# Four instead of three K tile pairs per block as seven products in the up projection, with the squared rectification on ScalarE and earlier transposes

## The chip, the cores and the metric

The kernel runs on one core of one Trainium2 chip. The metric is device time in microseconds (us). A core has TensorE (PE; its weight loads are listed as PEld), VectorE (DVE), ScalarE (ACT), GpSimd (POOL) and SyncE (SP), each with its own stream of instructions; here SP only issues DMAs. The engines hand work to each other by semaphores.

## What is computed

One encoder block for 256 tokens of width 2048, all in 32-bit floats: an input projection, two kinds of attention, an output projection with a layer norm, and a feed-forward part with a second layer norm. The change lies in the first half of the feed-forward part:

```python
x = _layer_norm(DEEPNORM_ALPHA * x + mix, ln1_g[l], ln1_b[l])
h = jnp.square(jax.nn.relu(x @ w_up[l])) @ w_down[l]      # w_up 2048 x 8192, w_down 8192 x 2048
x = _layer_norm(DEEPNORM_ALPHA * x + h, ln2_g[l], ln2_b[l])
```

## The kernel before

**Number format.** A 32-bit value is used as a sum of two rounded halves, hi and lo, and a product becomes three matmuls: hi·hi, hi·lo, lo·hi. A weight arrives by DMA in a raw tile of 2048 columns (two K tiles of 128 rows, a "pair"). ACT writes the rounded hi half of 1024 columns (line 389) and DVE then subtracts it from the raw value to get lo (line 390). The hi and lo tiles lie in five slots (NSLOT); the raw tiles in three buffers (NRAW), so the load of pair j+3 waits until the last split of pair j has read its buffer.

**The up projection.** Its 8192 columns are worked off in eight blocks of 1024. Block 0 goes by single tiles of 128 columns (ft 0 to 7). While ft 3, 4 and 5 end, DVE and ACT also prepare, once for all blocks, sums of the tokens' halves for each pair that will be treated as seven products (lines 1058, 364 to 369). Blocks 1 to 7 take eight pairs each, with the tokens as the stationary side and 512 columns at a time. An ordinary pair (pair_products) is 24 matmuls: two K tiles, two token halves, two column halves, three parts. A pair of the list UP_SEVEN (seven_products) is computed with seven instead of eight sub-products in the manner of Strassen and Winograd, 21 matmuls. For this DVE first forms sums of the weights' quarters (lines 400 to 402, weight_sums), and three and a half tiles of 1024 are split instead of two. Block 1 does this with pairs 3 and 5, blocks 2 to 7 with pairs 3, 5 and 6. Below, the two splits of an ordinary pair 4 are called 4.0 and 4.1, and the four of a seven-product pair 3 are 3a to 3d (3d is half as wide).

**PSUM.** A block has four accumulators of its own (cb) and, for the seven products, four more (mb, allocated at its first seven-product pair). The two groups of four banks change roles from block to block. The transposes of a block's result go to the banks that held its cb, and these are then the banks of the next block's mb.

**The end of a block.** After the last seven-product pair up_gather copies the four mb banks with ACT and adds them up with DVE (lines 1098 to 1108). up_finish then treats four quarters i of the result. For each, ACT copies the quarter's cb bank to memory (1120, "own"), DVE adds it to the gathered quarter (1121; in block 7 straight from PSUM, 1123), and one DVE instruction rectifies and squares (1124). After four empty steps PE transposes each quarter (1137) and ACT copies it back to where the down projection will read it (1131, back).

**Order of the work.** The order within each engine is written out by hand: the program emits the instructions in sequence and each engine runs its own in that order. After each group of matmuls unit() is called. It first advances every generator of the list side (up_gather and up_finish are such generators, and each yield is one step), and then emits up to two weight pieces. A split needs a free slot: it is emitted once the slot five splits earlier has been released by its matmuls. The weight sums need none. An ordinary pair has four units (after each K tile and token half), a seven-product pair also four (after each of its splits a to d). up_finish starts within pair 7, at the unit after 7.1's first token half; its four quarters are the units up to 0.0 of the next block, and the transposes come at the units from 1.1 (first half) to 2.0 (second half).

The lines that put the steps of a quarter into one unit are these:

```python
for i in range(4):
    ...
    nc.scalar.copy(c, pb)
    nc.vector.tensor_add(g, g, c)
    ...
    nc.vector.scalar_tensor_tensor(g, g, 0.0, g, op0=ALU.max, op1=ALU.mult)
    yield
for _ in range(4):
    yield
```

Of the kernel before, what the change touches and what calls it, by code (L numbers as in the profile page):

```python
# [11 lines left out]
AF = mybir.ActivationFunctionType  # L12
ALU = mybir.AluOpType

P = 128
# [24 lines left out]
STORED = (12, 9, 22, 25, 4, 7)  # L40


UP_PAIRS = (3, 5, 6)
UP_SEVEN = ((), (3, 5)) + 6 * (UP_PAIRS,)
NHELD = 4
STAGE_AT = 24
# [34 lines left out]
def kernel(  # L81
# [19 lines left out]
    nc = tc.nc  # L101
# [364 lines left out]
    for b in range(1, 8):  # L466
        j_block.append([])
        for kp in range(8):
            j_block[b].append(up_pair(b, kp))
            if b == 1 and kp in (2, 6):  # L470
                i = (2, 6).index(kp)
# [384 lines left out]
    pts = {}  # L856
# [174 lines left out]
    for i in range(2):  # L1031
        t = work.tile([P, 2048], F32R, tag="big", name=f"us{i}", bufs=2)
        up_sums += [sums_view(t[:, a:a + 1024]) for a in (0, 1024)]
    rest = []
    for ft in range(NSPLIT, NFT):
# [5 lines left out]
        for p in range(ft == NSPLIT, 2):  # L1041
# [7 lines left out]
            if p == 1:  # L1049
                up_evac(ft, pb)  # L1050
                i = ft - 3
                if rest:
                    rest.pop()()
                if 0 <= i < len(UP_PAIRS):

                    k = slice(2 * UP_PAIRS[i], 2 * UP_PAIRS[i] + 2)
                    xs = spare_flat[:, 0:512].rearrange("p (k t) -> p k t", k=2)
# [20 lines left out]
    def seven_products(job, x, k, sums, cb, mb, first, last):  # L1078
        for a, w, o, pb, alone in ((("x", 1, 0), 0, 0, cb[0][0], False), (("s", 3), 0, 512, cb[0][1], False),
                                   (("x", 0, 0), 1, 0, mb[0], True), (("s", 1), 1, 512, mb[1], True),  # L1080
                                   (("s", 0), 2, 0, mb[2], True), (("s", 2), 2, 512, mb[3], True),
                                   (("x", 1, 1), 3, 0, cb[1][0], False)):
            use(job, w + 1)
            if a[0] == "x":
                h, l = (x[:, k + a[1], i * S + a[2] * P:i * S + (a[2] + 1) * P] for i in range(2))
            else:
                h, l = (sums[:, a[1], i] for i in range(2))
            hi, lo = job.hi[w][:, o:o + 512], job.lo[w][:, o:o + 512]
            for x_part, w_part, fst, lst in ((h, hi, True, False), (h, lo, False, False), (l, hi, False, True)):
                nc.tensor.matmul(pb, x_part, w_part, start=alone and first and fst, stop=alone and last and lst)  # L1090
            if o or w == 3:
                free(job, (w,))
                unit()
# [16 lines left out]
    def up_finish(b, cb, tag, seven):  # L1110

        r = rr[b // 4][:, b % 4 * 8:b % 4 * 8 + 8]
        own = r.rearrange("p f t -> p (f t)")
        for i in range(4):
            g, pb = gathered[i], cb[i // 2][i % 2]
            if not seven:
                nc.scalar.copy(g, pb)
            elif b < 7:
                c = own[:, i * 512:(i + 1) * 512]
                nc.scalar.copy(c, pb)  # L1120
                nc.vector.tensor_add(g, g, c)
            else:
                nc.vector.tensor_add(g, g, pb)
            nc.vector.scalar_tensor_tensor(g, g, 0.0, g, op0=ALU.max, op1=ALU.mult)
            yield
        for _ in range(4):
            yield
        pts = []

        def back(i):  # L1130
            nc.scalar.copy(r[:, i % 2 * 4:i % 2 * 4 + 4, i // 2 * P:(i // 2 + 1) * P],
                           pts[i].rearrange("p (f t) -> p f t", f=4))

        for i in range(4):
            pts.append(tag(f"ut{b}{i}"))
            for f in range(4):
                nc.tensor.transpose(pts[i][:, f * P:(f + 1) * P], gathered[i][:, f * P:(f + 1) * P], ident)  # L1137
            if b < 7:
                back(i)
            yield  # L1140
        if b == 7:
            for i in (0, 2):
                back(i)
                back(i + 1)
                yield

    for b in range(1, 8):
        tag, other_tag = (bank, acc) if b % 2 else (acc, bank)
        cb = [[tag(f"u{b}{tb}{j}") for j in range(2)] for tb in range(2)]
        mb = None  # L1150
        for n in range(8):
            job = j_block[b][n]
            if b == 7 and n == 7:
                r_split(0)
            if n in UP_SEVEN[b]:
                if mb is None:
                    mb = [other_tag(f"v{b}{j}") for j in range(4)]
                last = n == UP_SEVEN[b][-1]
                seven_products(job, x1hl, 2 * n, up_sums[UP_PAIRS.index(n)], cb, mb, n == UP_SEVEN[b][0], last)
                if last:  # L1160
                    side.append(up_gather(mb))
            else:
                pair_products(job, x1hl, 2 * n, cb, n == 0, n == 7,
                              up_finish(b, cb, tag, bool(UP_SEVEN[b])) if n == 7 else None)
# [51 lines left out]
    for p in range(2):  # L1216
        cb = [[(acc, bank)[p](f"d{p}{tb}{j}") for j in range(2)] for tb in range(2)]
        mb = None
        for n, pair in enumerate(pairs[p][:32 if p == 0 else 32 - NHELD]):
            b = pair // 2  # L1220
            if n % 2 == 0:
                i = n // 2 + 1
# [166 lines left out]
```

## Time and profile before

| what | value |
|---|---|
| time, median of 3 runs | 1112.53 us (1112.09 to 1113.03) |
| span of the profiled execution | 1110.6 us; the median lies 1.9 us above it |
| busy: PE, DVE, ACT | 99%, 81%, 55% of the span |
| granted TensorE clock | 0.999 |
| blocks 1 to 7 of the up projection | from 461.19 to 763.55 us |
| DMA | 217.08 MB, 195 GB/s mean |

The profile is one execution, with times from the span's start. In a timeline a row has its start, its duration, the engine and line, the operation with the names of what it writes and reads, and a count; in brackets stands how long the engine had been idle before it and what ended that. Rows that follow each other closely overlap a little, since an instruction starts while its predecessor drains: the cost of one in a full queue is the distance between starts. The chain of waits is the run of work that ended last, in order of time, and pauses between its pieces are work of other lines too short to be listed.

### The profile page before, as it was taken

Reading aid. Unit: us, or ns where it says so; the run is one execution under the profiler, and the core shown is the slowest. Engines: PE = TensorE matmul, PEld = TensorE weight load, DVE = VectorE, ACT = ScalarE, POOL = GpSimd, SP = SyncE. Lnnn points to the kernel's source line nnn. Section 1 sums busy time; section 2 is a strip of 40 time slices with the busy share of each in tenths; the row PEclk is TensorE's granted clock in tenths of the full one; section 3 lists DMA queues with packets and bytes.
Section 4 is the critical chain, followed back from the end, with each engine's and each line's share of the span. In section 5 each row is a group of like instructions: output and inputs, shape, how many; then the busy total and the mean of one; then the engine's idle time right before and its main releaser. Section 6 shows DMA issues by size and latency. Waiting matters only on the chain.

```text
span 1110.6 us, 13644 instructions
## 1 busy us (share of the span) xinstructions
PE 1102.9 (99%) x5193; PEld 921.7 (83%) x5193; DVE 901.0 (81%) x1198; ACT 613.8 (55%) x793; POOL 9.6 (1%) x18
## 2 busy tenths in 40 slices
PE   9999999999999999999999999999999999999997
PEld 8888888888888889888888888888888888888885
DVE  6676684666656777898998999899999998999886
ACT  4445664535453446455656656656666673665650
POOL 0000000000000000000000000000000000000000
PEclk9999999999999999999999999999999999999999
DMA  8655365444465554566656756755656665656672
GB/s 306 222 205 192 119 228 184 145 168 161 144 258 197 199 198 152 189 216 207 222 166 213 221 158 193 221 168 180 223 191 195 204 213 196 215 189 200 204 251 104
DMA packets 92561, 217.08 MB, mean 195 GB/s; under 512 B 4177, under 2 KB 62545, under 8 KB 84433
## 3 DMA queue, kind: packets, MB, share of 16 engines
q1 hardware_dynamic: 92064, 215.64, 57.7%
q8 instruction: 40, 0.66, 0.2%
q10 hardware_dynamic: 432, 0.59, 0.2%
q14 instruction: 25, 0.20, 0.1%
HBM read 214.12 MB, written 2.10 MB: 195 GB/s over the span
## 4 chain that ended last, share of the span: by engine, by line
PE 96%; DVE 2%; DMA 1%; issue 0%; ACT 0%; POOL 0%; DVEq 0%; ACTq 0%; POOLq 0%
PE d L302 20%; PE u L302 18%; PE r L302 16%; PE o L302 8%; PE v L1090 5%; PE m L302 5%; PE s L1090 4%; PE u L1090 4%; PE d L1090 3%; PE up L734 2%; PE pu L734 2%; PE ut L1137 1%; PE pv L302 1%; PE up L740 1%; PE pu L740 1%; PE pq L302 1%
## 5 line engine op out<-in xcount | busy, mean ns | idle before, releaser
L302 PE MATMUL d<-hi_wd,rhl 128*128 128x512 f32 x664 | 182.9, 390 | 0.0
L389 ACT CAST hi_wu<-raw_wu 128x1024 fp32r<-128x1024 f32 x112 | 118.1, 1058 | 116.6 <-DVE raw_wu L401 57.9
L389 ACT CAST hi_wd<-raw_wd 128x1024 fp32r<-128x1024 f32 x125 | 130.0, 1052 | 75.8 <-PE d L302 33.5
L390 DVE TENSOR_TENSOR lo_wd<-raw_wd,hi_wd 128x1024 fp32r<-128x1024 f32 x125 | 148.6, 1220 | 18.2 <-ACT hi_wd L389 17.4
L302 PE MATMUL u<-hi_wu,x1hl 128*128 128x512 f32 x576 | 162.7, 393 | 0.0
L390 DVE TENSOR_TENSOR lo_wu<-raw_wu,hi_wu 128x1024 fp32r<-128x1024 f32 x112 | 133.3, 1220 | 23.4 <-ACT hi_wu L389 22.6
L302 PE MATMUL r<-hi_ret,xhl 128*128 128x512 f32 x512 | 147.1, 397 | 0.0
L302 PEld LDWEIGHTS d<-hi_wd,rhl 128*128 128x128 f32 x664 | 124.3, 188 | 25.7
L302 PEld LDWEIGHTS u<-hi_wu,x1hl 128*128 128x128 f32 x576 | 106.4, 188 | 20.9
L302 PEld LDWEIGHTS r<-hi_ret,xhl 128*128 128x128 f32 x512 | 93.9, 188 | 18.2
L302 PE MATMUL d<-lo_wd,rhl 128*128 128x512 f32 x332 | 102.6, 389 | 0.1
L191 DVE TENSOR_TENSOR lo_ret<-raw_ret,hi_ret 128x1024 fp32r<-128x1024 f32 x64 | 75.7, 1220 | 23.9 <-ACT hi_ret L190 23.7
L302 PE MATMUL u<-lo_wu,x1hl 128*128 128x512 f32 x288 | 88.9, 390 | 0.0
L302 PE MATMUL r<-lo_ret,xhl 128*128 128x512 f32 x256 | 79.4, 391 | 0.0
L190 ACT CAST hi_ret<-raw_ret 128x1024 fp32r<-128x1024 f32 x64 | 64.9, 1051 | 16.4 <-PE r L302 12.2
L302 PEld LDWEIGHTS d<-lo_wd,rhl 128*128 128x128 f32 x332 | 62.2, 188 | 13.4 <-DVE lo_wd L390 0.6
L302 PEld LDWEIGHTS u<-lo_wu,x1hl 128*128 128x128 f32 x288 | 54.1, 188 | 11.4
L302 PE MATMUL o<-hi_wo,mix 128*128 128x512 f32 x208 | 57.1, 392 | 0.0
L302 PEld LDWEIGHTS r<-lo_ret,xhl 128*128 128x128 f32 x256 | 48.1, 188 | 10.4
L191 DVE TENSOR_TENSOR lo_wo<-raw_wo,hi_wo 128x1024 fp32r<-128x1024 f32 x26 | 31.2, 1222 | 19.6 <-ACT hi_wo L190 18.9
L302 PEld LDWEIGHTS o<-hi_wo,mix 128*128 128x128 f32 x208 | 38.7, 188 | 7.8
L302 PE MATMUL m<-hi_mla,xhl 128*128 128x512 f32 (+1 forms) x168 | 42.5, 363 | 0.0
(297 smaller groups left out, 1908.6 us busy)
## 6 DMA issues: line engine op xcount, KB each, us to landing
raw_wu<-in_w_up SPq DMA_DIRECT2D x64, 1024.0 KB, 5.7
raw_wd<-in_w_down SPq DMA_DIRECT2D x64, 1024.0 KB, 5.5
raw_ret<-in_w_ret SPq DMA_DIRECT2D x32, 1024.0 KB, 4.8
raw_wo<-in_w_out SPq DMA_DIRECT2D x16, 1024.0 KB, 4.8
raw_mla<-in_w_mla SPq DMA_DIRECT2D x14, 672.0 KB, 4.7
raw_qk<-in_w_qk SPq DMA_DIRECT2D x8, 640.0 KB, 3.9
row<-in_ln_rows SPq DMA_DIRECT2D x4, 1024.0 KB, 4.7
raw_uv<-in_w_uv SPq DMA_DIRECT2D x2, 1024.0 KB, 4.7
```

The costliest lines, as they stand in the source:

```text
L190: nc.scalar.copy(hi[:, o:e], r)
L191: nc.vector.tensor_sub(lo[:, o:e], r, hi[:, o:e].bitcast(F32))
L302: nc.tensor.matmul(accs[j][:, :w], x_part, w_part[:, a:a + w], start=first and fst and i == 0, stop=last and lst and i == len(steps) - 1)
L389: nc.scalar.copy(h, src)
L390: nc.vector.tensor_sub(l, src, h.bitcast(F32))
L734: nc.tensor.matmul(pb, hi[:, a:a + P], hl[:, k0 + i], start=first and i == ks[0], stop=last and i == ks[-1])
L740: nc.tensor.matmul(pb[:, 0:S], lo[:, a:a + P], hl[:, k0 + i, 0:S], start=False, stop=last and i == ks[-1])
L1090: nc.tensor.matmul(pb, x_part, w_part, start=alone and first and fst, stop=alone and last and lst)
L1137: nc.tensor.transpose(pts[i][:, f * P:(f + 1) * P], gathered[i][:, f * P:(f + 1) * P], ident)
```

## The change

A pair 2 is added to the list of seven-product pairs, so blocks 2 to 7 have four of them (2, 3, 5, 6) and block 1 still has 3 and 5. The sums of the tokens are prepared for four pairs, at ft 3 to 6. In up_finish DVE's instruction of line 1124 is replaced by an ACT instruction that rectifies in place, at the same point of the program, and the copy back after the transposes becomes an ACT instruction that squares. Two of the four empty steps go, so the transposes are emitted two units sooner, from 1.0 (first half) to 1.1 (second half).

```diff
-UP_PAIRS = (3, 5, 6)
+UP_PAIRS = (2, 3, 5, 6)
 UP_SEVEN = ((), (3, 5)) + 6 * (UP_PAIRS,)
...
                 nc.vector.tensor_add(g, g, c)
             else:
                 nc.vector.tensor_add(g, g, pb)
-            nc.vector.scalar_tensor_tensor(g, g, 0.0, g, op0=ALU.max, op1=ALU.mult)
+            nc.scalar.activation(g, g, AF.Relu)
             yield
-        for _ in range(4):
+        for _ in range(2):
             yield
         pts = []

         def back(i):
-            nc.scalar.copy(r[:, i % 2 * 4:i % 2 * 4 + 4, i // 2 * P:(i // 2 + 1) * P],
-                           pts[i].rearrange("p (f t) -> p f t", f=4))
+            nc.scalar.activation(r[:, i % 2 * 4:i % 2 * 4 + 4, i // 2 * P:(i // 2 + 1) * P],
+                                 pts[i].rearrange("p (f t) -> p f t", f=4), AF.Square)
```

## The prediction

> **What bounds the kernel now.** The page comes first.
>
> ```profile
> span 1110.6 us, 13644 instructions
> PE 1102.9 (99%) x5193; PEld 921.7 (83%) x5193; DVE 901.0 (81%) x1198; ACT 613.8 (55%) x793; POOL 9.6 (1%) x18
> ```
>
> PE is always busy, so a matmul less is time less, as long as DVE keeps up. The chain of waits, in order of time, gives the price of a matmul and the length of a block.
>
> ```profile
> 477.51 1.36 PE u L1090 x6
> ...
> 492.47 20.40 PE u L302 x90
> ...
> 628.01 14.96 PE u L302 x66
> 643.41 1.40 PE u L302 x6
> 645.25 1.39 PE u L302 x6
> ...
> 651.66 1.36 PE u L1090 x6
> ...
> 671.38 14.96 PE u L302 x66
> ```
>
> 66 matmuls in 14.96 us are 0.2267 us each. Pair 7 begins at 628.01 and again at 671.38: a block takes 43.37 us. The four short pauses (643.41 + 1.36 to 645.25: 0.48) are the transposes, 1.9 us in all; 183 matmuls of 0.2267 are 41.5, and together that is the block: no wait of PE is left in it. The windows view tells how near DVE is in this stretch.
>
> ```profile
> 608.29:651.66 43.37, 43.37 (x201) 35.92 (x200) 39.16 (x43) 27.00 (x34) 0.00 (x0) 1.00 0.64 194
> ```
>
> The third pair of columns is DVE: 39.16 of 43.37 us. What it spends them on is in its timeline.
>
> ```profile
> 611.92 1.22 DVE L400 TENSOR_TENSOR t<-raw_wu 128x1024 f32<-128x1024 f32 x1
> ...
> 614.51 2.35 DVE L390 TENSOR_TENSOR lo_wu<-raw_wu,hi_wu 128x1024 fp32r<-128x1024 f32 x2
> ...
> 618.52 1.22 DVE L400 TENSOR_TENSOR t<-raw_wu 128x1024 f32<-128x1024 f32 x1
> ...
> 621.11 2.35 DVE L390 TENSOR_TENSOR lo_wu<-raw_wu,hi_wu 128x1024 fp32r<-128x1024 f32 x2
> ...
> 625.12 4.63 DVE L390 TENSOR_TENSOR lo_wu<-raw_wu,hi_wu 128x1024 fp32r<-128x1024 f32 x4
> ...
> 633.22 1.23 DVE L390 TENSOR_TENSOR lo_wu<-raw_wu,hi_wu 128x1024 fp32r<-128x1024 f32 x1 [1.06 <-ACT hi_wu L389]
> 634.36 0.69 DVE L1105 TENSOR_TENSOR rr<-rr 128x512 f32<-128x512 f32 x1
> ...
> 635.69 0.69 DVE L1121 TENSOR_TENSOR rr<-rr 128x512 f32<-128x512 f32 x1
> 636.41 0.69 DVE L1124 SCALAR_TENSOR_TENSOR rr<-rr 128x512 f32<-128x512 f32 x1
> 637.02 0.69 DVE L1108 TENSOR_TENSOR rr<-rr 128x512 f32<-128x512 f32 x1
> ...
> 645.13 0.69 DVE L401 TENSOR_TENSOR raw_wu<-raw_wu,t 128x512 f32<-128x512 f32 x1
> ```
>
> A lo costs 1.135 (four in 4.63, whose last drains 0.09), so an ordinary pair 2.27. Weight sums cost 2.59 (611.92 to 614.51), a whole seven-product pair 6.60 (611.92 to 618.52). An add of up_finish with its rectification costs 1.33 (635.69 to 637.02), two adds of up_gather as much (634.36 to 635.69).
>
> **The sum of busy time.** On PE the fourth pair saves 3 matmuls in each of six blocks: 6 x 3 x 0.2267 = 4.1 us; a block without waits would be 42.7. On DVE a block was 5 x 2.27 + 3 x 6.60 + 4 x 1.33 + 2.7 of up_gather = 39.2, as measured. Afterwards it is 4 x 2.27 + 4 x 6.60 + 4 x 0.66 (the add alone) + 2.7 = 40.8: the four rectifications given away (2.7) pay for most of the pair (4.3). On this count DVE has 1.9 us to spare per block, where it had 4.2, and the change gains 4.1. The count leaves out the order.
>
> **The wait that is added.** In up_finish ACT now does own copy 0, rectification 0, own copy 1, rectification 1 and so on, and rectification i needs DVE's add i, while add i+1 needs own copy i+1, which stands behind rectification i. Until now ACT ran through these copies without waiting for DVE. ACT's timeline at the same block end:
>
> ```profile
> 629.25 1.05 ACT L389 CAST hi_wu<-raw_wu 128x1024 fp32r<-128x1024 f32 x1 [0.82 <-DMA raw_wu<-in_w_up]
> ...
> 632.11 1.08 ACT L389 CAST hi_wu<-raw_wu 128x1024 fp32r<-128x1024 f32 x1
> 633.05 1.10 ACT L1120 COPY rr<-u 128x512 f32<-128x512 f32 x2
> ...
> 638.93 1.06 ACT L389 CAST hi_wu<-raw_wu 128x1024 fp32r<-128x1024 f32 x1 [1.66 <-PE u L302]
> 645.94 1.05 ACT L389 CAST hi_wu<-raw_wu 128x1024 fp32r<-128x1024 f32 x1 [5.95 <-DVE raw_wu L401]
> 646.89 1.06 ACT L1131 COPY rr<-ut 128x512 f32<-128x512 f32 x2
> ```
>
> The last two rows show what an ACT queue behind a DVE wait looks like: the first transpose was over before PE went on at 643.41, but its copy back ran at 646.89, behind a hi split that waited 5.95 us for weight sums. Handovers cost little: DVE's L401 ends at 645.82 and ACT starts at 645.94 (0.12); ACT's split ends at 633.19 and DVE starts at 633.22 (0.03). The own copies take 0.5 each in the queue, and about 0.6 until the result is there. A rectification isn't in the trace; the nearest rows of ScalarE and of the instruction replaced are these.
>
> ```profile
> L613 ACT ACTIVATE vg<-vg 128x512 f32<-128x512 f32 x4 | 2.5, 633 | 0.0
> ...
> L1124 DVE SCALAR_TENSOR_TENSOR rr<-rr 128x512 f32<-128x512 f32 x28 | 19.4, 692 | 1.0
> ```
>
> I take 0.63, or 0.5 in a full queue. The Trainium skill, ScalarE: Activation LUTs, Rules for kernel authors, sends relu to VectorE, which it says is up to about 3 times faster in bf16. By that rule a rectification would take some 2 us here, an estimate from the 692 ns, and the block walked below would grow by about another 6; in 32-bit floats the rows give the two engines the same speed, and I go by them.
>
> **Walking one block.** The second bound is the load of raw tiles: pair 1's load waits until 6b of the block before has read its buffer.
>
> ```profile
> DMA to landing us min/median/max: 5.6/5.7/7.6
> ```
>
> Here 6b's lo ended at 623.46 and the hi of 1.0 started at 629.25, released by the DMA: 5.8 later. Now the loop, in us after DVE is done with 6b. 5.8: hi of 1.0, then four copies of up_gather, then at 8.7 the hi of 1.1 (2.86 later, as 629.25 to 632.11). DVE: lo of 1.1 from 9.8, sums of pair 2, new at this place, to 13.5, two gather adds to 14.8, add 0 to 15.5. ACT, which has sat since own copy 0 (done by 10.3): rectification 0 at 15.6, own 1 to 16.7. DVE add 1 to 17.4; ACT rectification 1, hi 2a to 19.1, own 2 to 19.6; DVE lo 2a, add 2 to 21.0; ACT rectification 2, own 3 to 22.2; DVE add 3 to 22.9; ACT rectification 3, hi 2b to 24.6. From here DVE is never free: 2b, 2c, 2d to 27.5, sums 3 to 30.1, 3a to 3d (4.0) to 34.1, pair 4 to 36.4, pair 5 to 43.0, sums 6 to 45.6, 6a and 6b to 47.9. So the loop closes after 47.9 us, not 42.7.
>
> PE sees it as follows. It can start 6a at 46.8 - 47.9 = -1.1, needs 45 matmuls (10.2) for pairs 6 and 7, and enters the next block at 9.1. The third transpose, two units sooner than before, stands in PE's queue at 9.1 + 10.8 and waits for rectification 2 (21.7): 1.7. Block product 2b waits for the copy back of the first transpose, its PSUM bank, queued on ACT behind hi 2b and 2c: 0.6. 3a waits for its lo, behind sums 3: 1.9. 6a waits 0.6, and small waits make 0.4. That is 5.2 on 42.7: the same 47.9. What hid the handshake so far was PE's ordinary pair 2 (5.4 us) between the block end and pair 3; now the first two seven-product pairs, 13.2 us of DVE in 9.5 of PE, follow it directly.
>
> Block by block: 3 to 7 take 47.9 - 43.37 = 4.5 more each, 22.7. Block 2 is different, since block 1 gathers earlier.
>
> ```profile
> 504.60 2.35 DVE L390 TENSOR_TENSOR lo_wu<-raw_wu,hi_wu 128x1024 fp32r<-128x1024 f32 x2
> ```
>
> It starts at 492.47 + 48 x 0.2267 = 503.35 with up_gather already done but the lo of pair 1 only ready at 506.95. With add 0 then ahead of the sums I get rectification 3 some 0.6 sooner than in the later blocks: +4.0. Had DVE been fully ahead there, it would be about +1.
>
> **The token sums.** A fourth set at ft 6 lengthens a chain that is already a handshake. ACT's cast of the sums waits for DVE's, and the next weight splits stand behind it:
>
> ```profile
> 456.03 0.62 ACT L368 CAST us<-xm 128x512 fp32r<-128x512 f32 x1 [4.26 <-DVE xm L367]
> ```
>
> ```profile
> 450.59 2.36 DVE L191 TENSOR_TENSOR lo_wu<-raw_wu,hi_wu 128x1024 fp32r<-128x1024 f32 x2 [1.64 <-ACT hi_wu L190]
> ...
> 457.63 2.36 DVE L390 TENSOR_TENSOR lo_wu<-raw_wu,hi_wu 128x1024 fp32r<-128x1024 f32 x2 [1.64 <-ACT hi_wu L389]
> ...
> 461.31 2.36 DVE L390 TENSOR_TENSOR lo_wu<-raw_wu,hi_wu 128x1024 fp32r<-128x1024 f32 x2
> ...
> 471.18 1.22 DVE L400 TENSOR_TENSOR t<-raw_wu 128x1024 f32<-128x1024 f32 x1
> ...
> 473.77 2.35 DVE L390 TENSOR_TENSOR lo_wu<-raw_wu,hi_wu 128x1024 fp32r<-128x1024 f32 x2
> ```
>
> With sums a step takes 457.63 - 450.59 = 7.0, without them 3.7. The step to 461.31 becomes 7.0, so DVE arrives 3.4 later, and 0.6 more for the lo of the sums: 3a of block 1 is ready at 474.99 + 4.0 = 479.0 where PE wants it at 477.51. That is +1.5, between 0 (if DVE makes it up) and 2.6.
>
> The three other edits cost nothing: squaring instead of copying back is one ACT instruction for one; block 1 loses 2.7 us of DVE, which PE's ordinary pairs hid; in block 7 there is no own copy, so no handshake, and the next seven-product pair is the fifth of the down projection. Sum: 22.7 + 4.0 + 1.5 = +28.2, the 4.1 saved already in it. On the span 1138.8, on the median 1140.7, rounded 1140.
>
> **The rivals.** (1) The count of busy time is right and slack swallows the handshake: DVE's own waits stay under 1.9 us per block. Then -4.1 + 1.5 = -2.6, 1110, faster. For it: 40.8 against 42.7, and ACT far from full. Against it: the walk has 7.1 us of DVE waits per block (47.9 less 40.8). It decides once they are under 1.9, say if DVE came to add 0 some 5 us sooner than 14.8. (2) A softer form of the forecast: without the load of pair 1 on the loop DVE goes straight on from 6b and the loop is 46.2: 2.8 per block, 14 + 2.5 = +16.5, 1129. (3) Table loads:
>
> ```profile
> L613 ACT ACT_TABLE_LOAD x4 | 5.1, 1283 | 0.1
> ```
>
> If Relu and Square need different tables, ACT loads twice per block end. The load before Relu falls into ACT's wait for add 0; the one before Square delays hi 2d and the loop by 1.3: +7.7, 1148. The Trainium skill, ScalarE: Activation LUTs, Table sets: the hidden batching unit, has relu in every set as filler and doesn't name square there. By it one load would do for all, since the set with Square holds Relu too: +1.3.
>
> **How the numbers follow.** The forecast has 0.75, rival 1 0.11, rival 2 0.08, rival 3 0.06. A difference under 0.2%, 2.2 us, can't be told from none; 0.03 of rival 1 lies there. Low end: 1127, below rival 2. High end: 1150, with table loads, or with pair 1's load at 7.6 instead of 5.7 (1.9 x 5 = 9.5). Faster 0.08, same 0.03, slower 0.89.
>
> **What would show it.** Right: a block of about 47.9 in the chain; ACT's rectification idle some 8 us per block, waiting for DVE L1121; PE waiting at transposes for ACT and at lines 1090 for lo; DVE busy about 40.8 per block. Wrong: a block of 42.7 and no PE wait; an ACT_TABLE_LOAD beside Square or Relu; PE gaps outside blocks 1 to 7.

## The result, and the profile after

The changed kernel takes 1139.35 us (median of 4 runs, 1139.09 to 1139.67) against 1112.76 (1112.09 to 1113.03): 1.024 times the time, 95% interval 1.0227 to 1.0254. The profiled span went from 1110.6 to 1137.4 us, 26.8 more. The forecast was 1140. Ratios below are against the kernel before, run on the same chip.

From the page after: the span, the busy time of each engine, the shares of the chain that ended last, and the row of the new instruction:

```profile
span 1137.4 us, 13651 instructions
...
PE 1107.7 (97%) x5175; PEld 914.1 (80%) x5175; DVE 909.6 (80%) x1206; ACT 635.5 (56%) x834; POOL 9.6 (1%) x18
...
PE 65%; DVE 21%; ACT 6%; issue 4%; DMA 3%; POOL 0%; ACTq 0%; DVEq 0%; POOLq 0%
...
L1124 ACT ACTIVATE rr<-rr 128x512 f32<-128x512 f32 x28 | 17.6, 631 | 55.7 <-DVE rr L1121 49.9
```

The shares of the chain before were these:

```profile
PE 96%; DVE 2%; DMA 1%; issue 0%; ACT 0%; POOL 0%; DVEq 0%; ACTq 0%; POOLq 0%
```

There are 18 matmuls fewer, as promised, and DVE and ACT are about as busy in share as before (80% for 81%, 56% for 55%). What is new is in the last two rows of the page after: 35% of the chain doesn't run through PE, where it was 4%, and ACT's rectification, 631 ns long, has sat 55.7 us at the head of an idle engine, 49.9 of it waiting for DVE's adds of line 1121. Six blocks end this way (1 to 6; block 7 has line 1123 in its place), so that is 8.3 us each.

The chain of waits gives the length of a block. Line 400 here is the weight sums of pair 3:

```profile
570.36 1.23 DVE t L400
...
617.78 1.23 DVE t L400
...
665.18 1.23 DVE t L400
...
685.61 5.39 DMA raw_wu<-in_w_up
...
712.68 1.23 DVE t L400
```

Blocks now follow each other at 47.4 us (47.42, 47.40, 47.50), where it was 43.37, and the chain goes through DVE and the load of a raw tile. The windows view of one such period:

```profile
617.78:665.18 47.40, 44.06 (x198) 34.73 (x197) 40.72 (x45) 30.21 (x41) 0.00 (x0) 1.00 0.57 178
```

DVE is busy for 40.72 us of it, which is what the count of busy time said; it also idles for 6.7. ACT's timeline at the block end shows why (start, duration, line, names, count, and in brackets the idle time and what ended it):

```profile
643.60 1.06 ACT L389 CAST hi_wu<-raw_wu 128x1024 fp32r<-128x1024 f32 x1 [1.25 <-DMA raw_wu<-in_w_up]
...
646.47 1.07 ACT L389 CAST hi_wu<-raw_wu 128x1024 fp32r<-128x1024 f32 x1
647.42 0.61 ACT L1120 COPY rr<-u 128x512 f32<-128x512 f32 x1
653.35 0.63 ACT L1124 ACTIVATE rr<-rr 128x512 f32<-128x512 f32 x1 [5.32 <-DVE rr L1121]
653.89 0.57 ACT L1120 COPY rr<-u 128x512 f32<-128x512 f32 x1
655.21 0.63 ACT L1124 ACTIVATE rr<-rr 128x512 f32<-128x512 f32 x1 [0.76 <-DVE rr L1121]
...
658.67 0.63 ACT L1124 ACTIVATE rr<-rr 128x512 f32<-128x512 f32 x1 [1.41 <-DVE rr L1121]
...
660.54 0.63 ACT L1124 ACTIVATE rr<-rr 128x512 f32<-128x512 f32 x1 [0.76 <-DVE rr L1121]
661.07 1.03 ACT L389 CAST hi_wu<-raw_wu 128x1024 fp32r<-128x1024 f32 x1
```

Own copy, rectification, own copy, rectification: each rectification waits for DVE (5.32, 0.76, 1.41, 0.76), and the hi of 2b gets its turn only at 661.07. DVE's timeline is the other half of the same exchange:

```profile
652.63 0.68 DVE L1121 TENSOR_TENSOR rr<-rr 128x512 f32<-128x512 f32 x1
...
654.49 0.69 DVE L1121 TENSOR_TENSOR rr<-rr 128x512 f32<-128x512 f32 x1 [0.57 <-ACT rr L1120]
656.81 1.23 DVE L390 TENSOR_TENSOR lo_wu<-raw_wu,hi_wu 128x1024 fp32r<-128x1024 f32 x1 [1.64 <-ACT hi_wu L389]
...
659.81 0.69 DVE L1121 TENSOR_TENSOR rr<-rr 128x512 f32<-128x512 f32 x1 [1.17 <-ACT rr L1120]
662.14 1.23 DVE L390 TENSOR_TENSOR lo_wu<-raw_wu,hi_wu 128x1024 fp32r<-128x1024 f32 x1 [1.64 <-ACT hi_wu L389]
...
665.18 1.22 DVE L400 TENSOR_TENSOR t<-raw_wu 128x1024 f32<-128x1024 f32 x1
```

Add 1 waits for own copy 1, which stood behind rectification 0; lo 2a waits for hi 2a, behind rectification 1; and so on. From 0.57 + 1.64 + 1.17 + 1.64 come 5.0 of DVE's idle 6.7 us. On PE the loss arrives at four places per block, plus one in block 1:

```profile
706.86 0.66 PE L1137 MATMUL ut<-ident,rr 128*128 128x128 f32 x4 [1.42 <-ACT rr L1124]
...
711.10 0.50 PE L1090 MATMUL v<-hi_wu,x1hl 128*128 128x512 f32 x1 [0.34 <-ACT rr L1131]
...
716.54 0.50 PE L1090 MATMUL u<-lo_wu,x1hl 128*128 128x512 f32 x1 [1.39 <-DVE lo_wu L390]
...
732.01 0.50 PE L1090 MATMUL u<-lo_wu,x1hl 128*128 128x512 f32 x1 [0.21 <-DVE lo_wu L390]
```

```profile
478.82 0.50 PE L1090 MATMUL u<-lo_wu,x1hl 128*128 128x512 f32 x1 [1.28 <-DVE lo_wu L390]
```

They are the third transpose, product 2b, the lo of 3a and the lo of 6a. Counted between the starts of matmuls each costs some 0.16 more than its bracket (the first matmul behind a wait takes 0.50 us instead of 0.39): 3.4 in brackets make about 4.0 of the 4.7 us between 42.7 and 47.4. The other 0.7 wasn't followed to its places.

### The profile page after: what moved, and what is told of

It is laid out like the page before. It is cut to its first block, busy times and chain, and to the rows that moved or that the text cites. A ratio compares the mean times of both kernels' runs of the same rounds, so it can differ in the third digit from the quotient of the medians.

```text
span 1137.4 us, 13651 instructions
## 1 busy us (share of the span) xinstructions
PE 1107.7 (97%) x5175; PEld 914.1 (80%) x5175; DVE 909.6 (80%) x1206; ACT 635.5 (56%) x834; POOL 9.6 (1%) x18
## 4 chain that ended last, share of the span: by engine, by line
PE 65%; DVE 21%; ACT 6%; issue 4%; DMA 3%; POOL 0%; ACTq 0%; DVEq 0%; POOLq 0%
PE d L302 19%; PE r L302 15%; DVE lo_wu L390 9%; PE o L302 8%; PE m L302 4%; PE s L1090 4%; PE d L1090 3%; DMA raw_wu<-in_w_up 3%; DVE t L400 3%; ACT hi_wu L389 3%; PE pu L734 2%; DVE raw_wu L401 2%; DVE rr L1121 1%; DVE ut L402 1%; PE pv L302 1%
## 5 line engine op out<-in xcount | busy, mean ns | idle before, releaser
L302 PE MATMUL u<-hi_wu,x1hl 128*128 128x512 f32 x480 | 135.4, 393 | 0.0
L302 PEld LDWEIGHTS u<-hi_wu,x1hl 128*128 128x128 f32 x480 | 88.8, 188 | 17.5
L302 PE MATMUL u<-lo_wu,x1hl 128*128 128x512 f32 x240 | 74.1, 390 | 0.0
L1090 PE MATMUL v<-hi_wu,us 128*128 128x512 f32 x156 | 53.0, 394 | 0.0
L302 PEld LDWEIGHTS u<-lo_wu,x1hl 128*128 128x128 f32 x240 | 45.0, 188 | 9.4
L1124 ACT ACTIVATE rr<-rr 128x512 f32<-128x512 f32 x28 | 17.6, 631 | 55.7 <-DVE rr L1121 49.9
```

The source lines that it names most:

```text
L302: nc.tensor.matmul(accs[j][:, :w], x_part, w_part[:, a:a + w], start=first and fst and i == 0, stop=last and lst and i == len(steps) - 1)
L1124: nc.scalar.activation(g, g, AF.Relu)
```

## The experiments

The theory: the order of ACT's queue costs the time. Each rectification waits at the head of the queue for DVE, and the next own copy and the next hi splits, for which DVE waits in turn, stand behind it. The rivals: the fourth pair is simply too much for DVE; or the transposes two units sooner and their banks are what PE waits for; or only the long wait for add 0 matters.

**The rectifications one step later.** ScalarE still does them, ahead of the transposes, but behind the own copies and the splits 2a and 2b:

```diff
-            nc.scalar.activation(g, g, AF.Relu)
             yield
+        for i in range(4):
+            nc.scalar.activation(gathered[i], gathered[i], AF.Relu)
         for _ in range(2):
             yield
```

> The four rectifications stay on ScalarE and ahead of the transposes, but are emitted together one step later, behind all four own copies and the splits 2a and 2b. Theory (order of ACT's queue: each rectification holds back the next own copy and the next splits): the handshake is gone, DVE runs its adds without waiting, its loop is about 42.5 us against PE's 42.7 per block, and the time is 1111 us (1108 to 1116). Rival (amount of work: four pairs are too much for DVE, or the transposes two units sooner and the PSUM banks they hold are what PE waits for): nothing of that changes, 1139 us, or above 1130.

Measured: 1111.09 us (1110.5 to 1111.57), ratio 0.9986, 0.9977 to 0.9995. The same instructions on the same engines in another order take 28 us less. In its trace none of DVE's four adds waits for an own copy any more, and from block 1 to block 7 PE waits only for the 1.3 us in block 1 and for another 0.2.

**Both functions after the transposes.** The copy back rectifies from PSUM, and a second instruction squares in place:

```diff
-            nc.scalar.activation(g, g, AF.Relu)
             yield
...
-            nc.scalar.activation(r[:, i % 2 * 4:i % 2 * 4 + 4, i // 2 * P:(i // 2 + 1) * P],
-                                 pts[i].rearrange("p (f t) -> p f t", f=4), AF.Square)
+            q = r[:, i % 2 * 4:i % 2 * 4 + 4, i // 2 * P:(i // 2 + 1) * P]
+            nc.scalar.activation(q, pts[i].rearrange("p (f t) -> p f t", f=4), AF.Relu)
+            nc.scalar.activation(q, q, AF.Square)
```

> Nothing between DVE's add and the transpose; the copy back rectifies from PSUM and a further ACT instruction squares in place, so ACT does 28 instructions more and waits for no add of DVE. Theory (order of ACT's queue): 40.8 us of DVE and 42.7 of PE per block, time 1110 us (1107 to 1114), with the 1.3 us wait at pair 3 of block 1 left in it. Rival (amount of work, or the early transposes and their banks): 1139 us, or more, since ACT has 2 us more per block.

Measured: 1109.74 us (1109.01 to 1110.18), ratio 0.9973, 0.9962 to 0.9983. In its chain pair 7 begins every 42.7 us (its 54 matmuls are pairs 7, 0 and part of 1), and PE has no wait in a block:

```profile
542.34 12.24 PE u L302 x54
...
585.02 12.24 PE u L302 x54
...
627.71 12.24 PE u L302 x54
```

```profile
589.08:631.76 42.68, 42.68 (x198) 35.35 (x197) 40.38 (x44) 31.50 (x42) 0.00 (x0) 1.00 0.63 197
```

DVE is busy 40.4 us of 42.68: 95%, with four seven-product pairs and the early transposes, and PE doesn't wait. The first two rivals, too much work for DVE and the early transposes, fall with this.

**Four pairs with DVE's rectification.** In place of the two ScalarE functions the instruction of line 1124 and the copy back of the kernel before.

```diff
-            nc.scalar.activation(g, g, AF.Relu)
+            nc.vector.scalar_tensor_tensor(g, g, 0.0, g, op0=ALU.max, op1=ALU.mult)
...
```

> Four pairs as seven products and the transposes two units sooner, but rectification and squaring by one DVE instruction as before. Theory (order of ACT's queue): no handshake, but DVE's loop grows by four instructions of 0.7 us to about 45 us per block, so 1.7 us per block above the kernel before, 1124 us (1118 to 1130). Rival (amount of work on DVE decides): DVE has 2.7 us per block more than in the changed kernel, so slower than that, above 1140 us. Rival (early transposes and banks): about 1139 us.

Measured: 1122.81 us (1122.03 to 1123.52), ratio 1.0089, 1.0074 to 1.0104. DVE has more to do than in the changed kernel and the time is 16.5 us lower. DVE's own load does bound this version: a block takes 44.8 to 44.9 us, and DVE is busy for 43.1 of it. The removal of the four instructions is worth 13 us (against 1109.74), if it's done without the handshake.

**Three pairs, the rest as changed.**

```diff
-UP_PAIRS = (2, 3, 5, 6)
+UP_PAIRS = (3, 5, 6)
```

> ScalarE's rectification and the early transposes as in the changed kernel, but only three pairs as seven products. Theory (the handshake costs only what PE's ordinary pair 2 can't cover): by the same walk the loop is 43.4 us, which is PE's own 43.37; 1113 us (1111 to 1116). Rival (the handshake or the early transposes cost their 4 to 5 us per block wherever they stand): 1135 us or more.

Measured: 1115.24 us (1114.59 to 1116.3), ratio 1.0023, 1.0014 to 1.0032. The handshake alone is nearly covered by the ordinary pair 2. The weight sums of pair 3 in two successive blocks:

```profile
604.60 1.22 DVE L400 TENSOR_TENSOR t<-raw_wu 128x1024 f32<-128x1024 f32 x1
...
648.21 1.22 DVE L400 TENSOR_TENSOR t<-raw_wu 128x1024 f32<-128x1024 f32 x1
```

43.61 against PE's 43.37: the loop is a little longer than PE's block, where 43.4 was expected. Over all six blocks it is 2.1 us (262.3 between the first transposes of block 1 and of block 7, against 260.2 before), and another 1.0 is a wait of PE for a rectification at block 7's third transpose. Together that is about the 2.8 us above before.

**Own copies ahead.** In the changed kernel, copies 0 and 1 go into the first step, 2 and 3 into the second:

```diff
-                nc.scalar.copy(c, pb)
+                for k in (0, 1) if i == 0 else (2, 3) if i == 1 else ():
+                    nc.scalar.copy(own[:, k * 512:(k + 1) * 512], cb[k // 2][k % 2])
                 nc.vector.tensor_add(g, g, c)
```

> The changed kernel with own copies 0 and 1 in the first step and 2 and 3 in the second, so that an add no longer waits for the own copy behind the rectification before it; the rectifications still stand in ACT's queue ahead of the splits 2a and 2b. Theory (each wait of the handshake is on the loop and adds up): the four turns take 1.6 us less per block, six times, 1130 us (1127 to 1133). Rival (only the wait for add 0 at its head, 5 us, matters): 1139 us.

Measured: 1129.77 us (1129.56 to 1130.59), ratio 1.0155, 1.0141 to 1.0169. ACT's timeline has only two waits left for DVE's adds:

```profile
648.89 0.63 ACT L1125 ACTIVATE rr<-rr 128x512 f32<-128x512 f32 x1 [4.84 <-DVE rr L1122]
649.43 1.05 ACT L1121 COPY rr<-u 128x512 f32<-128x512 f32 x2
650.37 0.64 ACT L1125 ACTIVATE rr<-rr 128x512 f32<-128x512 f32 x1
...
653.84 1.23 ACT L1125 ACTIVATE rr<-rr 128x512 f32<-128x512 f32 x2 [1.89 <-DVE rr L1122]
```

The wait for add 0 is nearly as long as ever (4.84), and yet 9.6 us are gone, 1.6 a block. What counts is the sum of the turns on the loop.

**The load of pair 1 in two halves.**

```diff
+            v = raw.rearrange("p (f e c) -> p f e c", f=8, e=2)
+            if kp == 1:
+                for e in range(2):
+                    o = kp * 256 + e * P
+                    nc.sync.dma_start(v[:, :, e], w_up[8 * b:8 * b + 8, :, o:o + P].rearrange("f p c -> p f c"))
+            else:
...
```

> The changed kernel, with the load of pair 1 of each block issued as two DMAs of one K tile each, so that the hi of 1.0 waits for 512 KB only. Theory that this load is on the loop (hi of 1.0 is 1.3 us late for it in each of blocks 3 to 7): 1.3 us less per block, 1133 us (1131 to 1136). Rival (DVE and ACT alone close the loop, the load is beside it): 1139 us.

Measured: 1135.15 us (1134.78 to 1136.39), ratio 1.0206, 1.019 to 1.0221. The load was on the loop, but 4.2 us come back where 6.3 were expected. The chain shows what took its place:

```profile
615.73 1.23 DVE t L400
...
640.17 5.44 DMA raw_wu<-in_w_up
645.63 1.24 DVE t L400
...
662.11 1.23 DVE t L400
...
686.54 6.61 DMA raw_wu<-in_w_up
```

This period is 46.4 instead of 47.4, and its chain now runs through the next load: that of pair 2, whose weight sums (645.63) DVE starts when it lands. So 1.0 us comes back where 1.3 were expected, and in this profile in four of five periods only: the one that begins at 662.11 took 47.55, and there the load of pair 2 took 6.61 us instead of 5.44.

**The early transposes alone**, in the kernel before:

```diff
-        for _ in range(4):
+        for _ in range(2):
             yield
```

> The kernel before with two empty steps instead of four, all else unchanged: the transposes stand two units sooner in PE's queue. Theory (they are in nobody's way while DVE's rectification of the quarter is done in time): the last rectification would be ready some 0.5 us before its transpose or up to 0.4 after it, 1112.5 us (1112 to 1114). Rival (the early transposes are what costs): 1125 us or more.

Measured: 1112.03 us (1111.86 to 1112.28), ratio 0.9994, 0.9985 to 1.0003. PE waits for nothing in blocks 1 to 7 of its trace: the early transposes cost nothing where the rectification is done in time.

**The fourth set of token sums.** With the handshake out of the way the wait of 1.3 us at pair 3 of block 1 is what is left. First the sums of pair 2 were moved into block 1, on the same engines (in this run and the next the rectification and the square stand behind the transposes, as above, which is not shown again; pair_sums(i) holds the lines that prepare the sums of one pair):

```diff
-                if 0 <= i < len(UP_PAIRS):
...
+                if 0 <= i < len(UP_PAIRS) - 1:
+                    rest.append(pair_sums(i + 1))
...
+            if b == 1 and n == 6:
+                rest.append(pair_sums(0))
+            if b == 1 and n == 7:
+                rest.pop()()
```

> Both functions on ScalarE after the transposes, and the token sums of pair 2, which block 1 doesn't use, prepared within pairs 6 and 7 of block 1 instead of at the end of block 0. Theory (the sums at ft 6 lengthen a handshake of DVE and ACT there and PE waits 1.3 us at pair 3 of block 1): that wait goes and nothing takes its place, 1108.4 us (1107.5 to 1109.2), the whole saving of 4.1 us on PE. Rival (the wait at pair 3 has another cause, or moves with the sums into block 2): 1109.7 us or more.

Measured: 1114.01 us (1113.7 to 1114.81), ratio 1.0013, 1.0004 to 1.0022. A miss: 4.3 us more than with the sums where they were. ACT and PE in this run:

```profile
501.22 0.62 ACT L368 CAST us<-xm 128x512 fp32r<-128x512 f32 x1 [3.10 <-DVE xm L367]
```

```profile
PE ut L1140 <- DVE rr L1124: 3.7, 1, 3.7
```

The cast waits 3.1 us for DVE in front of up_gather's copies. DVE then idles 2.9 us for these copies and the split behind them (0.9 with the sums at ft 6), and its own part of the sums takes another 2.3 us there. PE waits 3.7 us, once, at the first transpose of block 2. In part it is the same fault, made anew: an instruction that waits, put ahead of work that others need. So the sums went to GpSimd, which has nothing to do there, with ACT's cast placed where they are long done and the lo part on GpSimd again:

```diff
+        nc.gpsimd.tensor_tensor(xs, x1hl[:, k, 0:S].bitcast(F32), x1hl[:, k, S:].bitcast(F32), op=ALU.add)
...
+            if b == 1 and n == 6:
+                next(pool)
```

Here next(pool) emits the cast and the lo part.

> Both functions on ScalarE after the transposes, and the token sums of pair 2 computed by the idle GpSimd from the start of block 1, with one cast by ACT before pair 6 of block 1. Theory (the fourth set costs only because DVE and ACT have it in their queues at a handshake): neither the 1.3 us wait at pair 3 of block 1 nor the 4 us wait of the run with the sums in block 1 is there, 1108.4 us (1107.6 to 1109.2). Rival (GpSimd's work slows DVE, or the cast holds back ACT's splits): 1109.7 us or more.

> The kernel with both functions after the transposes once more, beside the run with the sums on GpSimd on the same chip: 1109.7 us (1109 to 1110.2) again. If the 1.3 us wait in block 1 is what the other run takes away, this one lies 1.3 us above it; if the two are equal, that wait was not on the path.

Measured: 1108.32 us (1108.16 to 1109.66), ratio 0.9963, 0.995 to 0.9975, beside 1109.46 (1109.13 to 1110.37), ratio 0.9972, 0.9962 to 0.9983, with the sums at ft 6. The 1.1 us between them agree with the wait at pair 3, though the ranges of single runs overlap; in the profile of the version with GpSimd PE has no wait left from 431 to 800 us. Both versions are faster than both kernels; the one with GpSimd lies 4.7 us under the kernel before, which is the 4.1 us of saved matmuls and a rest that can't be told from noise.

## Why the prediction was right

The count of busy time promised 4.1 us, and the queue's order took it away and 27 more, as forecast. By its steps:

- A block of 47.9 us: measured 47.4. The walk had hi 1.0 5.8 us after DVE was done with 6b, add 0 at 14.8 and the last rectification at 23.0. In the rows above the load that 6b releases starts at 685.61, so at 638.2 a block earlier, and from there it is 5.4, 14.4 and 22.3: the load landed sooner than in the row that was taken (5.39 instead of 5.7), and that is most of the difference of 0.5.
- Five blocks at +4.5 and block 2 at +4.0: between the first transposes of successive blocks all six came out at +4.0 to +4.1, 24.4 us in all. What block 2 was to save rested on add 0 standing ahead of the sums of pair 2. In the trace it stands behind them there too (the sums start at 507.76, add 0 at 510.35), and block 2's rectifications wait like the others' (5.72, 0.76, 1.41, 0.76).
- PE's waits of 1.7, 0.6, 1.9 and 0.6: 1.6, 0.5, 1.55 and 0.4 counted between the starts of matmuls, in the places named.
- The token sums at +1.5: the wait is 1.44 between the starts of matmuls (1.28 in its bracket), and the first transposes of block 2 came at 511.75, against 510.11 with the sums on GpSimd: 1.6.
- The sum of +28.2 stands against 26.8 of span. The blocks were put 2.3 us too high, and 0.8 us came from places that the sum had at nothing: 0.4 of it is block 7's third transpose, which waits for a rectification (0.24 in its bracket) and comes 4.06 us behind the first instead of 3.66; the other 0.4 wasn't traced. So a part of the closeness is luck: the two errors have opposite signs. (The sum gave 1140.7, which rounds to 1141, not 1140.)
- Rival 1 needed DVE's waits to stay under 1.9 us per block: they were 6.7, and it is out. With both functions behind the transposes DVE idles for 42.68 - 40.38 = 2.3 us per block, and PE waits for none of it.
- Rival 2's softer loop of 46.2 was nearly reached when pair 1's load was halved (46.4).
- Rival 3 is out: no table load stands beside Relu or Square in any run here; the nine loads are those of before. The Trainium skill (ScalarE: Activation LUTs, Table sets: the hidden batching unit) says of relu that every set holds it, and that agrees.
- The rate of the rectification: 631 ns on ScalarE, against 692 ns on VectorE for rectification and squaring in one instruction, both for 128x512 in 32-bit floats. The rule of the Trainium skill (ScalarE: Activation LUTs, Rules for kernel authors) that relu belongs on VectorE comes with a figure for bf16, which no run here tests; in 32-bit floats these two rows show no such gap.

The prediction did not weigh that a remedy was at hand: both functions could stay on ScalarE, only later in its queue. Nor was block 7 free of the handshake, as it had it: there the rectifications wait for DVE's adds too (line 1123), and PE waited for one of them, 0.24 us in the changed kernel and 1.0 us in the run with three pairs.

## What to carry to other kernels

A sum of busy time per engine tells whether a change can win, not whether it will: before moving an instruction to an emptier engine, write down what is queued behind it there and who needs that. Where two engines hand work back and forth within one step, place the receiving instruction after everything that doesn't depend on it, as the late rectifications do, or where the handover has happened anyway, as behind the transposes. A handshake that is covered today can cost time as soon as the work that covers it is made shorter: here 0.35 us per block while pair 2 was ordinary (2.1 in six), and 4.7 once it had been shortened for PE and lengthened for DVE.

## What the runs showed of the hardware

One pause of PE cost more than its length. With the sums in block 1 PE paused for some 4 us, and the profile in windows of 3 us shows the granted TensorE clock (the column behind the engines) after it:

```profile
511.00:514.00 3.00, 0.00 (x0) 0.00 (x0) 2.93 (x4) 1.11 (x2) 0.00 (x0) 1.00 0.63 167
514.00:517.00 3.00, 2.83 (x12) 2.25 (x13) 3.00 (x6) 2.09 (x3) 0.00 (x0) 0.71 0.57 196
517.00:520.00 3.00, 3.00 (x15) 2.59 (x14) 2.71 (x4) 1.74 (x3) 0.00 (x0) 0.72 0.20 36
520.00:523.00 3.00, 3.00 (x17) 2.48 (x16) 2.82 (x4) 2.28 (x4) 0.00 (x0) 1.00 0.93 314
```

The two means of 0.71 and 0.72 hide a shorter and deeper fall: in windows of 1 us the granted clock is 0.63, 0.50, 0.50 and 0.67 from 515 to 519 us, and 1.00 before and after. From the first transpose to the fourth it took 7.11 us (514.17 to 521.28), against 5.55 with the sums on GpSimd, so the slow stretch cost 1.6 us on top of the pause. The many pauses of 1.4 us in the changed kernel left the clock at 1.00; no run shows from which length on it falls.

GpSimd's add is slow:

```profile
L1048 POOL TENSOR_TENSOR rr<-x1hl 128x512 f32<-128x512 f32 x1 | 1.8, 1780 | 6.9 <-DVE x1hl L890 6.9
```

It takes 1780 ns for what takes DVE 0.68 to 0.69 us. Nor was DVE left alone by it: while GpSimd wrote the lo part of the sums (498.47 to 500.43), DVE's add of line 1120 that began at 499.39 took 1.58 us, where the six others of that line take 0.68 to 0.69, and a lo of line 890 beside the sums took 0.87 instead of 0.69. PE waited for none of this, so it was the better place all the same.
